# A diffusion step of two layers on one core: one half of the first layer's gate g1 summed on VectorE during the input product

## The chip, the core and the metric

The kernel runs on one core of a Trainium2 chip. The core has TensorE (PE in the rows: matmuls; PEld is its weight load), VectorE (DVE), ScalarE (ACT), GpSimd (POOL) and SyncE (SP, which here issues nearly all loads). The metric is the device time of one execution in microseconds (us), as a median over runs. The rows of a profile call a place in the program by its line (L431 is line 431 of the kernel) and a tile by its name in the code.

## The reference, cut to what matters

Two groups of 128 tokens (context and latent, 256 columns in all) go through two layers of width 2048. Each layer has a mixer and a gated feed-forward part, and each of the two is modulated by vectors made from a conditioning vector (`c_ctx` for context, `c` for latent):

```
adaln(cvec, w, b) = silu(cvec) @ w + b            # w_ada[l]: 2048 x 12288
sh1, sc1, g1, sh2, sc2, g2 = split(adaln(...), 6) # 2048 each, once for c_ctx, once for c
h = rmsnorm(x) * (1 + sc1) + sh1
x = x + g1 * mixer(h)                             # layer 0: attention and a bidirectional scan
h = rmsnorm(x) * (1 + sc2) + sh2
x = x + g2 * conv_ffn(h)
```

In layer 0 the mixer is an input product (`h @ w_in`, 2048 x 6592), eight heads of differential attention, sixteen heads of an RWKV-7 scan in both directions, and an output product. What is changed is where the first 1024 of the 2048 values of layer 0's `g1` are summed. They are first used after the scan, in the residual of the output product.

## The kernel before, in words

**Products.** Every large product runs in `gemm`: a weight tile is loaded by SP into one of seven `raw` buffers (512 KB a load), ScalarE copies it to the high part of a `wbt` slot (L192), VectorE subtracts to get the low part (L194), and TensorE makes three matmuls for each 128 output channels (L252, L254, L255). There are four `wbt` slots, and a slot holds two steps of k where a group is 512 wide. A *turn* is one step of k: twelve matmuls in such a group. After each turn `gemm` calls a function `fill`.

**Gate vectors.** `w_ada` is 2 x 2048 x 12288, and each of the twelve segments is made in parts. After the input modulation, a part is a *half* of 1024 values. Both ways of making a half load sixteen tiles of 128 x 1024 (one for each step of k) into the same `raw` buffers.

- `ada_pe` lets TensorE do it: four matmuls per tile (L431), 64 in a half. The profile records each as two instructions, so a half is 128 records.
- `ada_vec` lets VectorE do it: two multiply-adds per tile into the tile `av` (L454 for the first tile, L456 for the other fifteen), then eight matmuls with a selector (L464, sixteen records) that sum over the partitions.

Both end in a transpose and an addition of the bias (L470, L482). The table `AS_VEC` names the halves that go the second way. One generator, `ada_gen`, walks a fixed list (`ada_order`): for layer 0 after the first modulation it is both halves of g1, then sc2, sh2, g2. `ada_step` advances it by one step, so the halves are made strictly in that order, at whatever pace the place that calls it sets.

**Order of the work around the change.** Layer 0's input product has a first part (`gemm_joint`, nine groups, with the modulation made beside it) and a second part (`gemm(p_in, ...)`, six groups of sixteen turns, 96 turns). In the second part the groups kb, vb and r come out through `in_evac`, and the attention heads and the normalisation `kk_norm` are small tasks that `step_tasks` advances by one piece each turn. Then comes the scan: `scores` for each pair of heads and direction, `solve(b)` for four batches (a triangular inverse by many small VectorE instructions and small matmuls), `apply`, and `post`. Here `scan_fill` calls `ada_step` at half a step each round until sh2 is done, and at five steps each round once the last scores are out. The last stretch of the scan, ahead of the output product, holds `solve(3)`, `subln` (the attention heads' normalisation, L1390 to L1401), and `post(1)` (L1351 to L1377). In `solve`, the tile `Xc` (L1207) ends a long run of VectorE instructions, and the matmuls of L1216 read it. Later, `fill_out` and `fill0` advance the generator in the output product and in the feed-forward part.

The program is written in one order, and a scheduler with a cost model places the instructions of each engine. So a change in one place can reorder others.

## Time and profile before

| what | value |
|---|---|
| median of three runs | 2709.16 us (2708.67 to 2729.94) |
| the profiled execution's own time | 2707.69 us |
| its span | 2705.6 us |
| PE, DVE, ACT, POOL busy in the span | 2615.6, 2020.5, 1258.5, 298.7 us |
| granted TensorE clock, mean | 0.977 |
| second part of the input product | 269 to 425 us |
| scan, to the start of the output product | 425 to 716 us |
| output product | 716 to 820 us |
| feed-forward part of layer 0 | 820 to 1580 us |

A row of a table by stretches gives the stretch, its length, then for each engine the busy time and the count of instructions, then the granted clock (1.00 is full), the share of time in which the DMA engines were busy, and GB/s. A row of a group gives line, engine, operation, tiles (output, then inputs), shape and count, then total busy us and the mean ns of one, then the idle time just before these instructions and what ended most of it. A row of the chain of waits gives when a piece began, how long it held the chain, and what it was. Durations of matmuls that follow each other overlap, so a group's busy time, not its mean, is what the engine spends on it.

### The profile page before, as it was taken

What the parts mean: (1) busy time and instruction counts of PE and PEld (TensorE: products, weight loads), DVE (VectorE), ACT (ScalarE), POOL (GpSimd) and SP (SyncE); (2) the same over time, 40 slices, a digit from 0 to 9 for tenths busy, and PEclk for the clock granted to TensorE, in tenths of its full rate; (3) what the DMA queues carried; (4) which work ended last, traced back from release to release, by engine and by line L of the source; (5) the groups of instructions that cost most, each with busy time, mean ns of one, the idle gap of its engine ahead of it and who ended that gap; (6) DMA issues with size and microseconds to landing.
All of it is one profiled execution on the core that took longest, in us unless ns stands there. A gap on an engine that the chain in (4) does not pass through costs nothing.

```text
span 2705.6 us, 60522 instructions
## 1 busy us (share of the span) xinstructions
PE 2615.6 (97%) x24347; PEld 2443.4 (90%) x24347; DVE 2020.5 (75%) x3468; ACT 1258.5 (47%) x2074; POOL 298.7 (11%) x313
## 2 busy tenths in 40 slices
PE   6999998999999999999999989999999999999998
PEld 5889996667898999999999989978889999999998
DVE  3457765767579998978999989996479985566655
ACT  3335654554345444434444454346344454355544
POOL 2000012011100000000000047653200000000000
PEclk8999999999799999999999989999999999999999
DMA  9997656655356887877878857865798876666653
GB/s 293 304 272 209 204 169 217 243 193 199 129 189 195 257 268 240 286 249 247 277 247 267 274 169 246 275 229 177 243 299 277 258 234 195 195 195 193 194 190 119
DMA packets 446969, 616.59 MB, mean 228 GB/s; under 512 B 33461, under 2 KB 317464, under 8 KB 446048
## 3 DMA queue, kind: packets, MB, share of 16 engines
q1 hardware_dynamic: 442288, 600.83, 70.2%
q0 software_dynamic: 3040, 6.57, 0.7%
q10 hardware_dynamic: 1360, 5.33, 0.5%
q8 instruction: 191, 3.13, 0.5%
q14 instruction: 90, 0.74, 0.1%
HBM read 604.75 MB, written 7.86 MB: 226 GB/s over the span
## 4 chain that ended last, share of the span: by engine, by line
PE 84%; DVE 7%; DMA 6%; ACT 1%; issue 1%; SPq 0%; POOL 0%; DVEq 0%; ACTq 0%; POOLq 0%
PE mm L255 22%; PE mm L252 22%; PE mm L254 22%; PE ada L431 4%; DVE cu L1655 3%; DMA raw<-in_w_ada 2%; DMA raw<-in_w_in 2%; PE mm L1087 1%; DVE wbt L194 1%; DMA raw<-in_w_up 1%; PE mm L304 1%; PE mm L306 1%; PE mm L305 1%; PE mm L1648 1%; PE mm L1120 1%
## 5 line engine op out<-in xcount | busy, mean ns | idle before, releaser
L192 ACT ACTIVATE wbt<-raw 128x1024 fp32r<-128x1024 f32 (+3 forms) x768 | 793.7, 1037 | 1035.4 <-PE mm L254 696.8
L252 PE MATMUL mm<-hbt,wbt 128*128 128x256 f32 x3888 | 1086.5, 282 | 6.0 <-ACT hbt L585 2.3
L254 PE MATMUL mm<-hbt,wbt 128*128 128x256 f32 x3888 | 1081.5, 280 | 2.7 <-DVE hbt L587 2.7
L194 DVE TENSOR_TENSOR wbt<-raw,wbt 128x1024 fp32r<-128x1024 f32 (+1 forms) x688 | 812.6, 1188 | 357.7 <-ACT wbt L192 345.5
L255 PE MATMUL mm<-hbt,wbt 128*128 128x256 f32 x3888 | 1064.2, 280 | 3.5 <-DVE wbt L194 3.3
L252 PEld LDWEIGHTS mm<-hbt,wbt 128*128 128x128 f32 x3888 | 733.3, 189 | 20.3 <-issue 9.2
L254 PEld LDWEIGHTS mm<-hbt,wbt 128*128 128x128 f32 x3888 | 734.0, 189 | 6.9 <-DVE hbt L587 4.7
L255 PEld LDWEIGHTS mm<-hbt,wbt 128*128 128x128 f32 x3888 | 723.2, 189 | 9.7 <-DVE wbt L194 4.7
L254 PE MATMUL mm<-u,wbt 128*128 128x256 f32 x1344 | 371.0, 278 | 0.0
L252 PE MATMUL mm<-u,wbt 128*128 128x256 f32 x1344 | 370.9, 278 | 0.0
L255 PE MATMUL mm<-u,wbt 128*128 128x256 f32 x1344 | 365.7, 278 | 0.0
L456 DVE SCALAR_TENSOR_TENSOR av<-raw,silu_c,av 128x1024 f32<-128x1024 f32 x270 | 337.2, 1278 | 29.6 <-DMA raw<-in_w_ada 29.5
L194 POOL TENSOR_TENSOR wbt<-raw,wbt 128x1024 fp32r<-128x1024 f32 x80 | 193.5, 2427 | 909.8 <-DMA raw<-in_w_pw 800.2
L252 PEld LDWEIGHTS mm<-u,wbt 128*128 128x128 f32 x1344 | 252.2, 188 | 0.4 <-issue 0.4
L254 PEld LDWEIGHTS mm<-u,wbt 128*128 128x128 f32 x1344 | 252.0, 188 | 0.4 <-issue 0.4
L255 PEld LDWEIGHTS mm<-u,wbt 128*128 128x128 f32 x1344 | 249.1, 188 | 0.4 <-issue 0.4
L431 PE MATMUL ada<-raw,silu_c 128*32 128x256 f32 (+2 forms) x2688 | 166.0, 337 | 31.3 <-DMA raw<-in_w_ada 15.6
L1655 DVE SCALAR_TENSOR_TENSOR cu<-mm,vec,cu 128x256 f32<-128x256 f32 x428 | 174.4, 470 | 2.2 <-ACT cu L1639 1.0
L1544 DVE SCALAR_TENSOR_TENSOR cv<-mm,vec,cv 128x254 f32<-128x254 f32 x344 | 147.3, 474 | 11.8 <-ACT cv L1539 11.8
L431 PEld LDWEIGHTS ada<-raw,silu_c 128*32 128x32 f32 x2688 | 70.3, 112 | 91.7 <-issue 26.2
L304 PE MATMUL mm<-hbt,wbt 128*128 128x256 f32 x304 | 91.7, 302 | 1.9 <-DVE qkv L311 1.0
L1539 ACT ACTIVATE cv<-mm,vec 128x256 f32<-128x256 f32 x172 | 72.0, 474 | 45.9 <-PE mm L255 45.8
(449 smaller groups left out, 2889.6 us busy)
## 6 DMA issues: line engine op xcount, KB each, us to landing
raw<-in_w_ada SPq DMA_DIRECT2D x384, 512.0 KB, 5.3
raw<-in_w_up SPq DMA_DIRECT2D x688, 256.0 KB, 4.2
raw<-in_w_down SPq DMA_DIRECT2D x168, 512.0 KB, 5.0
raw<-in_w_pw SPq DMA_DIRECT2D x128, 256.0 KB, 4.3
raw<-in_w_in SPq DMA_DIRECT2D x128, 192.0 KB, 6.1
raw<-in_w_in SPq DMA_DIRECT2D x48, 512.0 KB, 3.9
raw<-in_w_out SPq DMA_DIRECT2D x32, 512.0 KB, 4.0
raw<-in_w_pw SPq DMA_DIRECT2D x32, 512.0 KB, 4.7
```

The lines of the kernel that those rows point to most:

```text
L192: act.activation(w[:, 0, 0:na * n], v, AF.Copy)
L194: pl.lo(pl.count).tensor_tensor(out=w[:, 1, 0:na * n], in0=v, in1=w[:, 0, 0:na * n].bitcast(F32), op=ALU.subtract)
L252: pe.matmul(ps, lhsT=hi, rhs=r[:, 0:TT], start=(ki == 0 and (nl > 0 or j % 2 == 0)), stop=False, skip_group_check=True)
L254: pe.matmul(ps, lhsT=hi, rhs=r[:, TT:2 * TT], start=False, stop=False, skip_group_check=True)
L255: pe.matmul(ps, lhsT=lo, rhs=r[:, 0:TT], start=False, stop=(ki == nk - 1), skip_group_check=True)
L304: pe.matmul(ps, lhsT=hi, rhs=r[:, 0:TT], start=(i == 0), stop=False, skip_group_check=True)
L305: pe.matmul(ps, lhsT=hi, rhs=r[:, TT:2 * TT], start=False, stop=False, skip_group_check=True)
L431: pe.matmul(ps[32 * j:32 * j + 32, 0:nb * 32], lhsT=silu_c[:, kt, :], rhs=rv[:, j], start=(kt == 0), stop=(kt == KT - 1))
L456: dve.scalar_tensor_tensor(out=av[:, s], in0=raw, scalar=sc, in1=av[:, s], op0=ALU.mult, op1=ALU.add)
L1539: act.activation(o, ps, AF.Copy, scale=w(1, ct))
L1544: dve.scalar_tensor_tensor(out=o[:, :, a_], in0=v2(ps)[:, :, b_], scalar=w(k, ct), in1=o[:, :, a_], op0=ALU.mult, op1=ALU.add)
L1655: dve.scalar_tensor_tensor(out=o, in0=pads[a](k), scalar=V("w_dw", k * KT + ct), in1=o, op0=ALU.mult, op1=ALU.add)
```

## The change

`(0, "g1", 0)` joins the table `AS_VEC`, so the first half of layer 0's g1 is made by `ada_vec`. The generator now starts it in the second part of the input product: from the tenth turn on, every second turn takes one step until that half is done. The half takes 38 steps, so it runs from turn 10 to turn 84 of 96; `ada_until` after the product would finish it there if it were not done. When the scan begins, the generator stands at the second half of g1, and the scan has five halves to make in place of six.

```
-    AS_VEC = [(l, nm, i) for l, nm in ((0, "g2"), (1, "sc1"), (1, "sh1"), (1, "g2")) for i in range(2)] + [(1, "g1", 0)]
+    AS_VEC = [(l, nm, i) for l, nm in ((0, "g2"), (1, "sc1"), (1, "sh1"), (1, "g2")) for i in range(2)] + [(0, "g1", 0), (1, "g1", 0)]
...
         nrm_[0] = w1.enter_context(scoped("nrmg", 1))
-        gemm(p_in, hb, in_evac, step_tasks)
+        turns = [0]
+
+        def fill_in():
+            turns[0] += 1
+            if turns[0] % 2 == 0 and turns[0] > 8 and (0, "g1", 0) not in ada_done:
+                ada_step()
+            step_tasks()
+        gemm(p_in, hb, in_evac, fill_in)
+        ada_until(0, "g1", 0)
         drain()
```

Eight lines are added ahead of the scan's code, so L1207 before is L1215 after, and so on for every line behind it. Three places show how the instructions move.

TensorE, the last two scores of the scan, before (`X`, `W` are the inverse of batch 2; `th`, `kd`, `bk` belong to the scores; `ada` is a gate half):

```order
L431 MATMUL ada<-raw,silu_c 32x256 x9
L1282 MATMUL mm<-X_7742,W 64x64 x16
L1087 MATMUL mm<-kr,th 128x256 x4
L1087 MATMUL mm<-kr,kd 128x256 x4
L1098 MATMUL mm<-table,s0r_5212 128x128
L1101 MATMUL mm<-table,bk 128x128
L1102 MATMUL mm<-table,bk 128x128
L431 MATMUL ada<-raw,silu_c 32x256
L1291 MATMUL mm<-W,X_7742 64x64 x16
```

The same place after:

```order
L1290 MATMUL mm<-X_7819,W 64x64 x16
L1095 MATMUL mm<-kr,th 128x256 x4
L1095 MATMUL mm<-kr,kd 128x256 x4
L1106 MATMUL mm<-table,s0r_5289 128x128
L1109 MATMUL mm<-table,bk 128x128
L1299 MATMUL mm<-W,X_7819 64x64 x16
L1110 MATMUL mm<-table,bk 128x128
```

Ten gate matmuls are gone from here. The gate halves of the scan are the same sequence shifted by one, so up to this place both kernels have a gate half at the same spots, and it is the last 64 matmuls that are missing.

TensorE, around the first matmuls that read `Xc` of the last `solve`, before (`sq`, `ones` are `subln`; `y`, `ex` belong to `post` and `subln`):

```order
L1390 MATMUL mm<-ones,sq 128x2 x4
L1351 MATMUL mm<-y,table 128x256
L431 MATMUL ada<-raw,silu_c 32x256 x8
L1390 MATMUL mm<-ones,sq 128x2 x4
L431 MATMUL ada<-raw,silu_c 32x256 x12
L1216 MATMUL mm<-Xc,W 32x16 x32
L858 MATMUL mm<-table,ex 128x128 x2
L1360 MATMUL mm<-table,sq 128x2 x2
L1351 MATMUL mm<-y,table 128x256
L431 MATMUL ada<-raw,silu_c 32x256 x4
L1229 MATMUL mm<-Gc,P_8629 16x16 x32
```

The same place after:

```order
L1398 MATMUL mm<-ones,sq 128x2 x4
L1224 MATMUL mm<-Xc,W 32x16 x32
L1359 MATMUL mm<-y,table 128x256
L1398 MATMUL mm<-ones,sq 128x2 x4
L1237 MATMUL mm<-Gc,P_8606 16x16 x32
L858 MATMUL mm<-table,ex 128x128
L1368 MATMUL mm<-table,sq 128x2 x2
L1359 MATMUL mm<-y,table 128x256
```

The first L1351 and the second four of L1390 stood ahead of the readers of `Xc` and now stand behind them (as L1359 and L1398).

VectorE at the same time, before (`Xc` is the tile waited for, `rn` a norm of `subln` that needs ScalarE in between):

```order
L1194 TENSOR_TENSOR ft<-G,M_8547 128x512
L1353 SCALAR_TENSOR_TENSOR y<-mm,y 128x256
L1197 TENSOR_REDUCE G<-ft 128x8x8
L1201 TENSOR_SCALAR G_8599<-G,table 128x16x16
L1393 TENSOR_SCALAR rn<-mm 128x16
L1204 STREAM_TRANSPOSE Gc<-G_8599 128x16x2x16
L1395 RECIPROCAL rn<-rn 128x16
L1207 STREAM_TRANSPOSE Xc<-Gc 128x512
L1224 COPY P_8629<-mm 32x256
```

The same place after:

```order
L1202 TENSOR_TENSOR ft<-G,M_8563 128x512
L1205 TENSOR_REDUCE G<-ft 128x8x8
L1209 TENSOR_SCALAR G_8585<-G,table 128x16x16
L1212 STREAM_TRANSPOSE Gc<-G_8585 128x16x2x16
L1215 STREAM_TRANSPOSE Xc<-Gc 128x512
L1333 TENSOR_TENSOR y<-mm,y 128x256
L1338 TENSOR_TENSOR so<-mm,Sp 64x64 x2
```

L1353, L1393 and L1395 stood ahead of `Xc` and now stand behind it, and so do two of the four updates of `y` and `so` (L1325 and L1330 before). In turn four low parts of weights (L194) stand ahead of `Xc` where there were three.

In the second part of the input product, VectorE gets sixteen pairs of `av` among the low parts of the weights, SP gets sixteen loads of `w_ada` among those of `w_in` and of the attention caches, and TensorE gets the eight selector matmuls in the last group. The last matmuls of the attention heads stand at the same place among the product's as before.

## Prediction

> **What bounds the kernel now.** I read the page first: the busy times and the chain of waits (the work that ended last, followed back).
>
> ```profile
> span 2705.6 us, 60522 instructions
> ...
> PE 2615.6 (97%) x24347; PEld 2443.4 (90%) x24347; DVE 2020.5 (75%) x3468; ACT 1258.5 (47%) x2074; POOL 298.7 (11%) x313
> ...
> PE 84%; DVE 7%; DMA 6%; ACT 1%; issue 1%; SPq 0%; POOL 0%; DVEq 0%; ACTq 0%; POOLq 0%
> PE mm L255 22%; PE mm L252 22%; PE mm L254 22%; PE ada L431 4%; DVE cu L1655 3%; DMA raw<-in_w_ada 2%; DMA raw<-in_w_in 2%; PE mm L1087 1%; DVE wbt L194 1%; DMA raw<-in_w_up 1%; PE mm L304 1%; PE mm L306 1%; PE mm L305 1%; PE mm L1648 1%; PE mm L1120 1%
> ```
>
> TensorE is busy nearly all the time and holds the chain for 84% of the span; the gate matmuls (L431) alone hold 4%. On the average any matmul taken away should pay. But averages don't say what the removed ones are worth, so I look at the two stages that the change touches. First the price of a half on either engine, from the groups by shape (all of TensorE):
>
> ```profile
> L431 PE MATMUL ada<-raw,silu_c 128*32 128x256 f32 x1408 | 119.5, 405 | 11.0 <-DMA raw<-in_w_ada 10.3 <-DVE atr L470 0.6
> ...
> L464 PE MATMUL ada<-av,sel 128*32 128x256 f32 x144 | 11.1, 388 | 0.0
> ```
>
> and the groups of VectorE from 900 to 1150 us, where the feed-forward part makes halves this way:
>
> ```profile
> L456 DVE SCALAR_TENSOR_TENSOR av<-raw,silu_c,av 128x1024 f32<-128x1024 f32 x67 | 83.7, 1277 | 6.4 <-DMA raw<-in_w_ada 6.4
> ...
> L454 DVE TENSOR_SCALAR av<-raw,silu_c 128x1024 f32<-128x1024 f32 x4 | 2.8, 738 | 0.0
> ```
>
> On TensorE a half is 128 records of 119.5 / 1408 = 0.085 us, 10.9 us. In the new form TensorE still does 16 records of 11.1 / 144 = 0.077 us, 1.2 us, and VectorE gets 30 x 1.277 + 2 x 0.738 = 39.8 us.
>
> **What is added: the input product.** Stretches of the trace (its second part without its first turns, the densest 110 us of that, and two stretches of the feed-forward part that make halves on VectorE):
>
> ```profile
> 285.00:425.00 140.00, 140.00 (x1171) 137.66 (x1173) 84.17 (x149) 72.62 (x141) 18.08 (x43) 1.00 0.59 168
> 300.00:410.00 110.00, 110.00 (x915) 107.87 (x914) 70.81 (x125) 59.01 (x112) 11.43 (x29) 1.00 0.61 175
> 900.00:1150.00 250.00, 250.00 (x2128) 247.65 (x2127) 229.15 (x287) 117.63 (x160) 0.00 (x0) 1.00 0.83 262
> 1200.00:1250.00 50.00, 48.00 (x401) 47.15 (x400) 42.24 (x48) 19.97 (x23) 0.00 (x0) 1.00 0.79 249
> ```
>
> TensorE is busy 140.00 of 140 us, so the 1.2 us of L464 lie on the path: +1.2. VectorE goes from 84.17 to 124 us of 140, 89%. At 900 to 1150 us it is busy 229.15 of 250, 92%, with the same rhythm (one `av` instruction every second turn, one low part every second turn), and TensorE loses nothing. That row is nearest, so I take 0 for the contention. The other bound is the row from 1200 us, where TensorE lost 2.00 of 50 us: 2.00 / 50 x 140 = 5.6 us. What hides the 39.8 us are the four `wbt` slots of two turns each: 1171 records in 140 us are 0.12 us each, a turn of twelve 1.4 us, so the split may be 11.5 us late. If that is used up, each further `av` costs its 1.28 us. An `av` also waits in VectorE's queue for its load, with low parts of weights queued behind it; in 250 us these waits were 6.4 us (the L456 row), and TensorE stayed at 250.00.
>
> The sixteen loads (512 KB each, 8.4 MB) fill the DMA share, 0.59 at 168 GB/s, by 60 GB/s to about 0.8, under the 0.83 of 900 to 1150 us: 0. On SP's queue they stand among the loads of the attention caches (L758), which wait for attention matmuls and hold back all loads behind them; that is the rival below. POOL is moved past nothing. L470 and L482 run on VectorE in the last turns and nobody waits for them before the scan's end.
>
> **What is removed: the end of the scan.** Since the sequence of halves is shifted by one, the missing matmuls are the last 64, all after 650 us. The chain of waits there (x18 are 18 records):
>
> ```profile
> 650.37 1.41 PE ada L431 x18
> ...
> 656.19 0.55 PE ada L431 x2
> ...
> 669.27 1.00 PE ada L431 x16
> ...
> 673.61 1.00 PE ada L431 x16
> ...
> 677.08 1.28 ACT L1394
> ...
> 678.62 0.25 DVE rn L1395
> 678.87 0.58 DVE Xc L1207
> ...
> 679.50 1.19 PE mm L1216 x64
> ...
> 681.40 0.58 PE mm L1351 x2
> 681.97 1.01 PE ada L431 x8
> ...
> 684.75 0.65 PE mm L1360 x4
> 685.40 1.86 PE ada L431 x16
> 687.26 2.16 PE mm L1216 x64
> ...
> 691.41 1.50 PE mm L1390 x8
> ...
> 714.50 0.85 PE mm L1351 x2
> ...
> 715.78 0.21 PE mm L252
> ```
>
> and VectorE's timeline ahead of `Xc` (start, us, and in brackets the idle time before):
>
> ```profile
> 663.13 1.23 DVE L194 TENSOR_TENSOR wbt<-raw,wbt 128x1024 fp32r<-128x1024 f32 x1
> ...
> 666.78 0.41 DVE L1325 TENSOR_TENSOR y<-mm,y 128x256 f32<-128x256 f32 x1
> 667.11 0.45 DVE L1330 TENSOR_TENSOR so<-mm,Sp 64x64 f32<-64x64 f32 x2
> ...
> 675.17 0.42 DVE L1353 SCALAR_TENSOR_TENSOR y<-mm,y 128x256 f32<-128x256 f32 x1
> ...
> 676.79 1.06 DVE L1204 STREAM_TRANSPOSE Gc<-G 128x512 f32<-128x512 f32 x1
> 678.62 0.25 DVE L1395 RECIPROCAL rn<-rn 128x16 f32<-128x16 f32 x1 [0.78 <-ACT rn L1394]
> 678.79 0.65 DVE L1207 STREAM_TRANSPOSE Xc<-Gc 128x512 f32<-128x512 f32 x1
> ```
>
> Up to the last scores the gate matmuls are on the path: 1.41 + 0.55 = 1.96 us. From there to `Xc` the stage is VectorE's: the last `solve` runs as one unbroken row of instructions, and the gate matmuls of 669 to 677 us fill time in which TensorE would otherwise wait for `Xc`. They are worth 0 there. The new order shortens VectorE's row: two pairs of L1325 and L1330 go behind (0.8 each, 1.6), L1353 goes (0.4), and the wait for L1395 goes (`Gc` ends at 677.85, `Xc` starts at 678.79: 0.9), while one more L194 comes (1.2). That is 1.7 us. So `Xc` comes 1.96 + 1.7 = 3.7 us earlier.
>
> Behind `Xc` the granted clock decides (stretches of 5 us; the second column of numbers is TensorE's busy time, the third last is the clock):
>
> ```profile
> 675.00:680.00 5.00, 2.67 (x61) 1.58 (x62) 3.48 (x8) 2.93 (x6) 0.52 (x2) 1.00 1.02 406
> 680.00:685.00 5.00, 5.00 (x129) 3.76 (x124) 2.23 (x6) 1.97 (x5) 0.92 (x4) 0.68 1.05 386
> 690.00:695.00 5.00, 5.00 (x80) 4.21 (x79) 2.98 (x6) 3.18 (x7) 2.21 (x6) 0.50 0.49 181
> ...
> 715.00:720.00 5.00, 5.00 (x41) 4.85 (x40) 2.32 (x6) 2.33 (x6) 0.29 (x1) 0.91 0.00 0
> ```
>
> After the thin stretch at 675 to 680 us (2.67 busy of 5) the clock falls to half at about 681.8 us and stays there until the output product begins. L1216 takes 1.19 us before and 2.16 after the fall. TensorE works without a gap in this stretch, so here it is the bound, at half speed. By parts:
> - the 24 gate records gone from it: -1.01 - 1.86 = -2.9;
> - the first L1351 and the second L1390, which stood ahead of `Xc`, now run here: +0.85 + 1.50 = +2.35;
> - the clock falls earlier, since nothing fills the time before `Xc`: the work of 679.50 to 681.97 at half speed costs 0 to 2.3; I take +1.8, near the upper end, since the gap grows;
> - L1395 with its 1.28 us of ScalarE (L1394) now lies between L1390 and L858: 0 to 1.5, I take +0.7;
> - L1360 and L1351 come forward from the output product: 0.65 + 0.85 here, about half of it back at full speed there: +0.75.
>
> Together +2.7. The end of the scan is worth -3.7 + 2.7 = -1.0 us, between -4.0 (clock and L1395 at their lower ends, 2.5 less, and 0.5 for rounding) and +0.6.
>
> [...]
>
> Sum: +1.2 + 0 - 1.0 = +0.2 us on the profiled execution's own 2707.69, 2707.9. The median of the runs shown, 2709.16, lies 1.5 above that execution, so the forecast is 2709.4 us. From the output product on, both kernels do the same work in almost the same order: 0.
>
> **The rivals.**
> - *The freed time is paid in full*: TensorE holds 84% of the chain, the later stages absorb nothing, and all 128 records count: -10.9 + 1.2 = -9.7, 2699.5 us. For it speaks the first page; against it the rows at 669 to 677 us, which lie beside VectorE's work.
> - *The weights come late in the input product (slower)*: the cache loads on SP already wait (the queue's own waits, 285 to 430 us):
>
> ```profile
> SPq L758 <- PE mm L824: 8.3, 4, 3.9
> ```
>
>   With VectorE at 89%, the attention pieces that free these buffers come later, and the `w_in` loads behind them too. It decides once the split is more than 11.5 us late. The price is up to 8.3, if these waits reach TensorE once, plus 5.6 for the contention: 13.9, which gives 2723. Against it: in the densest 110 us VectorE would need 70.81 + 39.8 = 110.6, full but not far over, and the last attention matmuls keep their place.
> [...]
>
> That the change does not do what it says I exclude: the order of the instructions shows the half moved.
>
> **How the numbers follow.** Forecast 0.55 (its own range 2705 to 2715), paid in full 0.2, late weights 0.2 (spread over 2712 to 2723), clock 0.05. The range 2699 to 2718 leaves out the clock, the upper half of the late weights and a little of the full pay, together under 0.2. A measurement of this kernel can tell about 1% (27 us) from no change. Faster by over 1% needs more than all the gains together: 0.01. Slower by over 1% needs most of the 39.8 us of VectorE on the path: 0.02. Within 1%: 0.97.
>
> **What would show it.** Right: TensorE still 140 of 140 us in the input product with VectorE near 124; L431 with 1280 records in place of 1408; `Xc` some 3.7 us earlier against the last scores' place less what the input product adds; the clock at 0.50 from well before the first L1216 reader; the output product beginning within 2 us of before. Wrong: idle time of L252 to L255 put down to L194 or to `raw<-in_w_in` between 285 and 425 us (late weights), or an output product that begins 8 us or more earlier (full pay), or a clock of 1.00 between 690 and 710 us.

## The result, and the profile after

The changed kernel takes 2735.25 us (median, 2729.06 to 2759.87), the kernel before 2709.16. The ratio on record is 1.0077, with a 95% interval of 1.0048 to 1.0106 (the quotient of the two medians is 1.0096): slower by 0.8 to 1.0%. Disturbed runs are left out of all ratios here. The profiled execution takes 2733.12 us. From its page:

```profile
span 2731.3 us, 60324 instructions
...
PE 2618.5 (96%) x24235; PEld 2452.1 (90%) x24235; DVE 2054.2 (75%) x3500; ACT 1259.4 (46%) x2074; POOL 300.0 (11%) x313
```

The groups of the gate matmuls, by shape:

```profile
L431 PE MATMUL ada<-raw,silu_c 128*32 128x256 f32 x1280 | 107.1, 396 | 13.7 <-DMA raw<-in_w_ada 13.1 <-DVE atr L470 0.6
...
L464 PE MATMUL ada<-av,sel 128*32 128x256 f32 x160 | 12.8, 388 | 0.0
```

TensorE's work hardly changed (2618.5 us busy, 2615.6 before). The span grew by 25.7 us. Where, is seen by cutting both executions at the same places of the program: the input product's second part, the scan up to the last matmuls of L1087, and from there to the output product. First before, then after (the second number after the stretch's length is TensorE's busy time, the third last the clock):

```profile
269.12:424.77 155.65, 155.65 (x1297) 152.81 (x1295) 98.53 (x184) 83.00 (x164) 19.25 (x44) 1.00 0.62 183
275.00:325.00 50.00, 50.00 (x408) 48.35 (x407) 36.81 (x80) 29.79 (x68) 4.36 (x8) 1.00 0.66 194
424.77:654.68 229.91, 221.66 (x2970) 153.50 (x2971) 154.22 (x398) 116.75 (x315) 28.54 (x76) 0.99 0.62 209
654.68:715.43 60.75, 57.84 (x802) 45.14 (x799) 36.32 (x84) 25.90 (x53) 9.03 (x26) 0.72 0.58 213
```

```profile
267.58:443.80 176.22, 160.53 (x1313) 155.97 (x1311) 134.87 (x220) 83.22 (x164) 19.20 (x44) 0.95 0.68 208
443.80:674.17 230.37, 220.95 (x2952) 153.12 (x2953) 154.25 (x398) 117.14 (x315) 28.36 (x76) 0.99 0.61 206
674.17:743.78 69.61, 61.46 (x698) 53.42 (x695) 36.92 (x84) 26.36 (x55) 9.43 (x27) 0.56 0.21 72
```

The input product is 20.6 us longer, the scan 9.3 (0.5 + 8.8). The product begins 1.5 us earlier, so the output product begins 28.4 us later; 2.7 us come back behind it, which wasn't followed up.

**The input product.** TensorE does 4.9 us more work (160.53 - 155.65) and idles 15.7 (176.22 - 160.53). By stretches of 10 us of the changed kernel, all idle time lies in one place (the last row is one of the undisturbed ones):

```profile
285.00:295.00 10.00, 9.20 (x72) 8.39 (x71) 9.68 (x10) 5.80 (x11) 0.00 (x0) 1.00 0.90 302
295.00:305.00 10.00, 0.00 (x0) 0.00 (x0) 9.95 (x23) 2.72 (x12) 1.80 (x3) 0.67 0.81 245
305.00:315.00 10.00, 5.62 (x27) 5.66 (x28) 4.59 (x12) 1.22 (x3) 0.00 (x0) 0.50 0.20 61
...
345.00:355.00 10.00, 10.00 (x88) 10.00 (x87) 9.89 (x18) 6.33 (x15) 1.27 (x2) 1.00 0.67 199
```

The waits of 280 to 325 us name it, and VectorE's timeline shows what stood ahead:

```profile
PE mm L816 <- DVE a L810: 15.2, 1, 15.2
...
ACT e L800 <- DVE mx L796: 6.2, 1, 6.2
```

```profile
295.53 0.68 DVE L795 TENSOR_REDUCE mx<-mm 128x2 f32<-128x512 f32 x1
...
297.72 2.47 DVE L456 SCALAR_TENSOR_TENSOR av<-raw,silu_c,av 128x1024 f32<-128x1024 f32 x2
...
302.03 0.16 DVE L796 TENSOR_SCALAR mx<-mx 128x4 f32<-128x4 f32 x1
...
304.66 2.47 DVE L456 SCALAR_TENSOR_TENSOR av<-raw,silu_c,av 128x1024 f32<-128x1024 f32 x2
...
308.89 0.74 DVE L810 SCALAR_TENSOR_TENSOR a<-e,sm,a 128x128 f32<-128x128 f32 x2
```

An attention head goes back and forth between VectorE (L796), ScalarE (L800) and VectorE (L808, L810), and TensorE then transposes its result (L816). L796 needs 0.16 us, and its input is ready at 296.2; it runs at 302.0, behind `av`, a low part of weights and results of kb. L810 follows at 308.9. All product matmuls behind L816 in TensorE's order stop with it, though their weights lie ready (in the whole product TensorE waits for a weight once, 0.5 us). In VectorE's queue L796 was held 5.8 us with nothing else missing. The wait costs a second time: the clock is at 0.67 in the 10 us without a matmul, and at 0.50 from 305 to 315 us. The 4.9 us of extra work are the selector matmuls (1.2 by the prediction's price) and this half clock. The scheduler did not keep the half to the tenth turn and later, either: its first pair of `av` runs at 269.3 us, in the product's second turn.

**The end of the scan.** The same cut by 5 us, then ScalarE's timeline, then TensorE's, all of the changed kernel:

```profile
675.00:680.00 5.00, 2.84 (x37) 2.28 (x35) 3.76 (x8) 2.80 (x4) 0.00 (x0) 1.00 0.68 283
680.00:685.00 5.00, 4.65 (x23) 3.76 (x24) 2.15 (x8) 1.01 (x4) 0.52 (x1) 0.57 0.00 0
...
735.00:740.00 5.00, 5.00 (x35) 4.25 (x34) 1.59 (x3) 1.01 (x2) 0.59 (x2) 0.50 0.00 0
740.00:745.00 5.00, 4.69 (x27) 3.89 (x26) 3.29 (x9) 2.18 (x5) 1.59 (x5) 0.79 0.18 52
```

```profile
677.75 2.15 ACT L1166 ACTIVATE f<-W 32x512 f32<-32x512 f32 x2 [0.48 <-PE mm L1299]
679.93 0.37 ACT L1112 ACTIVATE s0T<-mm,th 128x128 f32<-128x128 f32 x1
```

```profile
680.35 0.53 PE L1123 MATMUL mm<-s0T,kr 128*128 128x128 f32 x2 [2.51 <-ACT s0T L1112]
...
690.37 1.12 PE L1326 MATMUL mm<-W,sf 128*64 128x128 f32 x8 [1.99 <-ACT sf L1320]
...
710.67 0.48 PE L858 MATMUL mm<-table,ex 128*128 128x128 f32 x1 [1.76 <-POOL ex L857]
```

Before, ScalarE made `s0T` ahead of `f`:

```profile
656.23 0.37 ACT L1104 ACTIVATE s0T<-mm,th 128x128 f32<-128x128 f32 x1 [2.75 <-PE mm L1102]
...
658.92 2.19 ACT L1158 ACTIVATE f<-W 32x512 f32<-32x512 f32 x2 [0.48 <-PE mm L1291]
```

Now `f` (2.15 us, of the last `solve`) stands ahead of it, and L1110, the last of the three transposes ahead of `s0T`, stands behind the 32 records of L1299. TensorE waits 2.51 us for `s0T`, no gate matmul fills the gap, and the clock falls at the last scores. It stays at half for some 61 us, to 742, where it was 34 us before (682 to 716).

### The profile page after: what moved, and what is told of

Read it like the earlier page. It is cut to its first block, busy times and chain, and to the rows that moved or that the text cites. A ratio compares the mean times of both kernels' runs of the same rounds, so it can differ in the third digit from the quotient of the medians.

```text
span 2731.3 us, 60324 instructions
## 1 busy us (share of the span) xinstructions
PE 2618.5 (96%) x24235; PEld 2452.1 (90%) x24235; DVE 2054.2 (75%) x3500; ACT 1259.4 (46%) x2074; POOL 300.0 (11%) x313
## 4 chain that ended last, share of the span: by engine, by line
PE 86%; DMA 6%; DVE 5%; ACT 1%; issue 1%; SPq 0%; DVEq 0%; POOL 0%; ACTq 0%
PE mm L252 22%; PE mm L254 22%; PE mm L255 22%; PE ada L431 4%; DMA raw<-in_w_ada 3%; DVE wbt L194 2%; PE mm L1095 1%; DMA raw<-in_w_in 1%; DMA raw<-in_w_up 1%; PE mm L304 1%; PE mm L306 1%; PE mm L305 1%; PE mm L1656 1%; DVE av L456 1%; PE mm L1128 1%
## 5 line engine op out<-in xcount | busy, mean ns | idle before, releaser
L252 PE MATMUL mm<-hbt,wbt 128*128 128x256 f32 x3888 | 1088.2, 283 | 6.0 <-ACT hbt L585 2.3
L255 PE MATMUL mm<-hbt,wbt 128*128 128x256 f32 x3888 | 1067.8, 281 | 4.1 <-DVE wbt L194 4.1
L194 DVE TENSOR_TENSOR wbt<-raw,wbt 128x1024 fp32r<-128x1024 f32 (+1 forms) x688 | 812.7, 1189 | 331.6 <-ACT wbt L192 319.5
L252 PEld LDWEIGHTS mm<-hbt,wbt 128*128 128x128 f32 x3888 | 736.6, 190 | 20.9 <-issue 9.5
L255 PEld LDWEIGHTS mm<-hbt,wbt 128*128 128x128 f32 x3888 | 726.4, 190 | 9.7 <-DVE wbt L194 5.5
L456 DVE SCALAR_TENSOR_TENSOR av<-raw,silu_c,av 128x1024 f32<-128x1024 f32 x300 | 374.5, 1280 | 41.0 <-DMA raw<-in_w_ada 40.7
L252 PE MATMUL mm<-u,wbt 128*128 128x256 f32 x1344 | 371.2, 278 | 0.0
L255 PE MATMUL mm<-u,wbt 128*128 128x256 f32 x1344 | 365.9, 278 | 0.0
L194 POOL TENSOR_TENSOR wbt<-raw,wbt 128x1024 fp32r<-128x1024 f32 x80 | 193.6, 2426 | 910.9 <-ACT wbt L192 908.4
L252 PEld LDWEIGHTS mm<-u,wbt 128*128 128x128 f32 x1344 | 252.3, 188 | 0.4 <-issue 0.4
L254 PEld LDWEIGHTS mm<-u,wbt 128*128 128x128 f32 x1344 | 252.1, 188 | 0.4 <-issue 0.4
L255 PEld LDWEIGHTS mm<-u,wbt 128*128 128x128 f32 x1344 | 249.2, 188 | 0.4 <-DVE wbt L194 0.4
L431 PE MATMUL ada<-raw,silu_c 128*32 128x256 f32 (+2 forms) x2560 | 154.5, 332 | 34.3 <-DMA raw<-in_w_ada 19.5
L431 PEld LDWEIGHTS ada<-raw,silu_c 128*32 128x32 f32 x2560 | 67.2, 114 | 90.1 <-DMA raw<-in_w_ada 27.2
```

Source lines behind the costliest of these rows:

```text
L194: pl.lo(pl.count).tensor_tensor(out=w[:, 1, 0:na * n], in0=v, in1=w[:, 0, 0:na * n].bitcast(F32), op=ALU.subtract)
L252: pe.matmul(ps, lhsT=hi, rhs=r[:, 0:TT], start=(ki == 0 and (nl > 0 or j % 2 == 0)), stop=False, skip_group_check=True)
L254: pe.matmul(ps, lhsT=hi, rhs=r[:, TT:2 * TT], start=False, stop=False, skip_group_check=True)
L255: pe.matmul(ps, lhsT=lo, rhs=r[:, 0:TT], start=False, stop=(ki == nk - 1), skip_group_check=True)
L431: pe.matmul(ps[32 * j:32 * j + 32, 0:nb * 32], lhsT=silu_c[:, kt, :], rhs=rv[:, j], start=(kt == 0), stop=(kt == KT - 1))
L456: dve.scalar_tensor_tensor(out=av[:, s], in0=raw, scalar=sc, in1=av[:, s], op0=ALU.mult, op1=ALU.add)
```

## The experiments

The table puts the traces side by side, in us. Input: the second part of the input product. The next three columns count from the scan's first gate matmul: to the end of the last scores (their last matmul), to the first reader of the last `Xc`, to the output product. All are worked out from TensorE's timelines. Ratio: time against the kernel before, with its interval. Each trace is one execution; in one set of 31 executions the kernel before took 2699.58 to 2742.41 us, so a trace's columns and the ratio need not agree to some 10 us.

| kernel | input | last scores | Xc | output | ratio |
|---|---|---|---|---|---|
| before | 155.6 | 236.8 | 254.7 | 290.7 | 1 |
| changed | 176.2 | 241.7 | 259.6 | 300.0 | 1.0077 (1.0048 to 1.0106) |
| give_room | 178.4 | 239.0 | 254.9 | 294.3 | 1.0112 (1.0041 to 1.0183) |
| no_loads | 190.9 | 238.0 | 254.0 | 294.2 | one time, 2735.85 us |
| twice_as_fast | 187.1 | 241.3 | 254.0 | 301.4 | one time, 2764.97 us |
| late_start | 161.8 | 252.1 | 268.0 | 307.6 | 1.0062 (1.0036 to 1.0088) |
| swap_half | 176.8 | 249.0* | 267.0* | 304.3* | 1.0026 (0.9991 to 1.0060) |
| late_swap | 160.4 | 248.6 | 265.4 | 306.1 | 1.0037 (1.0000 to 1.0074) |
| late_even | 169.6 | 238.2 | 256.1 | 293.5 | 1.0025 (0.9986 to 1.0063) |
| copies_first | 178.2 | 232.7 | 255.6 | 290.6 | 1.0061 (1.0022 to 1.0100) |
| combo | 166.4 | 231.6 | 249.6 | 289.0 | 1.0031 (0.9995 to 1.0066) |
| more_halves | 155.6 | 249.7* | 268.4* | 308.8* | 1.0033 (0.9987 to 1.0078) |
| warm_once | 155.6 | 249.9* | 267.9* | 303.0* | 0.9984 (0.9946 to 1.0022) |
| rate4 | 155.6 | 234.8 | 250.3 | 286.4 | 0.9960 (0.9925 to 0.9996) |
| rate4_again | 155.6 | 232.6 | 246.6 | 289.9 | 0.9957 (0.9914 to 1.0001) |
| late_rate4 | 160.4 | 233.9 | 249.8 | 289.0 | 1.0018 (0.9986 to 1.0049) |

In the rows with a star the clock also fell to half in mid-scan for some 27 us, which costs about 13 us (to the last scores 249.9 in warm_once, 236.8 before; last section); their later columns are read less 13.

### The input product: place, load or transfers?

**give_room.** Is it the place of L816 in TensorE's order?

```
-            yield
+            for _ in range(7 if h == 3 else 1):
+                yield
             ps = bank()
             for i in range(3):
                 pe.transpose(ps[:, i * P:(i + 1) * P], ...
```

> The changed kernel, but one head's attention (the fourth) waits 12 turns longer in program order between making its weights a on VectorE and turning them on TensorE: L816 stands at turns 32 and 33 of the input product on TensorE where it stood at 16 to 17.6. VectorE's work is the same, all is computed. Theory A (TensorE stops because this matmul stands in its fixed order ahead of weights that VectorE reaches 15 us later): the wait of 15.2 us for a goes, the half clock after it too, the scan begins at 425 to 430 us instead of 443.8, and the execution takes 2714 to 2720 us, since the end of the scan stays as in the changed kernel. Rival B (VectorE's 40 us cost TensorE some 18 us in the input product wherever the attention matmul stands, through late weights or buffers): waits of the same sum turn up elsewhere between 280 and 440 us, 2728 to 2735 us.

Measured: 178.4 us. The one wait of 15.2 became two, 8.5 and 7.6 us, both again for `a` (by the same matmul, L817 in this kernel), ending at 327 and 336 us. So theory A in this form falls. VectorE is behind by about 15 us, and TensorE meets that at the next thing VectorE owes it.

**no_loads.** VectorE's time, or the sixteen loads?

```
-            raw, nxt = nxt, (load(kt + 1) if kt < KT - 1 else None)
+            raw, nxt = nxt, (nxt if (l, nm, b0) == (0, "g1", 0) else
+                             load(kt + 1) if kt < KT - 1 else None)
```

> The changed kernel, but the half that VectorE makes in the input product reads its first load sixteen times: 15 of its 16 loads (7.9 MB) are left out, and the gate it makes is not the reference's. VectorE's instructions are the same in number and size. Theory A2 (VectorE's time): TensorE still waits 10 to 18 us for a in the first third of the input product, which takes 172 to 178 us (176.2 in the changed kernel). Rival B (the loads: raw buffers and transfers that the weights lack): the wait is gone, 156 to 162 us.

The waits of 280 to 330 us:

```profile
PE mm L816 <- DVE a L810: 22.7, 2, 15.7
```

Without the loads it is worse, 190.9 us, with a longer wait than expected. The loads aren't the cause (rival B falls). But this kernel changed more than the loads: its VectorE instructions are the same in number and not in place. First the changed kernel, then no_loads:

```profile
L456 DVE SCALAR_TENSOR_TENSOR av<-raw,silu_c,av x30: 1271/1280/1287, 280.6 to 388.3; 128x1024 f32<-128x1024 f32 x30
```

```profile
L456 DVE SCALAR_TENSOR_TENSOR av<-raw,silu_c,av x30: 1253/1276/1282, 269.3 to 328.2; 128x1024 f32<-128x1024 f32 x30
```

The same thirty instructions lie within 59 us in place of 108, denser than in twice_as_fast below (279.2 to 353.4). So 190.9 us belongs with the dense cases, and the loads with VectorE's load held fixed were not tested.

**twice_as_fast and late_start.** The dose: all 40 us of VectorE in half the turns, or at the old pace in a later place.

```
-            if turns[0] % 2 == 0 and turns[0] > 8 and ...
+            if turns[0] > 8 and ...                           # twice_as_fast
+            if turns[0] % 2 == 0 and turns[0] > 32 and ...    # late_start
```

> The changed kernel, but a step in every turn from turn 10 on, not in every second; all is computed. Theory A2 (local overload of VectorE): over 275 to 325 us VectorE would get 36.8 + 0.91 x 50 = 82 us of work for 50, so TensorE waits 25 to 35 us instead of 15.2 in the input product, again for a or for weights, and the product takes 184 to 196 us. Rival B (the place of one attention matmul in the fixed order, not the load, sets the loss): the wait stays between 12 and 18 us, 173 to 179 us.

> The changed kernel, but the half's steps begin behind turn 32 of the input product instead of behind turn 8, at the same pace; all is computed. Theory A2 (VectorE is overloaded locally: between 275 and 325 us it had 36.8 us of other work before, and one step of 1.28 us every second turn of 1.4 us adds 0.46 x 50 = 22.8, together 59.6 us for 50; TensorE waits for the first thing VectorE owes it, wherever that stands): from turn 32 on VectorE had 63 us in the last 110, with the half 103, so the wait of 15 us is gone, the input product takes 156 to 161 us (155.6 before, 176.2 in the changed kernel) and the scan begins near 427. The end of the scan stays at 294 to 300 us from its first gate matmul, since its fillers are still missing: 2712 to 2720 us where no other fall of the clock lies in the scan. Rival B (any 40 us of VectorE in this part costs TensorE some 18): input product 172 to 178 us.

The waits of twice_as_fast (270 to 350 us), then two stretches of late_start, then one of combo, which starts behind turn 36 with three steps in four turns:

```profile
PE mm L816 <- DVE a L810: 22.5, 3, 21.1
```

```profile
264.19:426.00 161.81, 157.41 (x1313) 153.03 (x1311) 135.33 (x222) 83.99 (x166) 25.75 (x49) 1.00 0.72 227
304.00:354.00 50.00, 50.00 (x415) 48.94 (x414) 45.90 (x69) 26.05 (x48) 3.62 (x6) 1.00 0.74 237
```

```profile
316.00:376.00 60.00, 55.53 (x464) 54.38 (x462) 59.96 (x83) 31.41 (x62) 2.35 (x4) 1.00 0.83 265
```

The input product grows with the density: 155.6 without the half, 160.4 to 161.8 late and slow, 166.4 and 169.6 late and denser, 176.2 as in the change, 187.1 at twice its pace. With VectorE at 45.90 of 50 us TensorE lost nothing (50.00 busy); at 59.96 of 60 it lost 4.5 (55.53 busy). So A2 holds: it is the local overload, met through the attention's chain. Whether the order on VectorE alone would do, with the attention's short instructions put ahead of `av`, was not tried. A turn takes 155.65 / 96 = 1.62 us, so one step of 1.277 us every second turn is 0.39 us per us. Between 275 and 325 us VectorE had 36.81 us of 50 before; with 19.7 more it needs 56.5. (The expectations used 1.4 us a turn and came to 59.6, a little much.) The whole of late_start was not cured: its input product is just over the 156 to 161 us expected, the scan takes 307.6 where 294 to 300 were expected, and the time is 2730.91 us for 2712 to 2720. Six steps were left behind the last turn. In the scan's first 60 us TensorE idles 12.1 us (7.8 before), mostly where gate matmuls wait for their own loads, and the clock is at half there for some 17 us. combo's input product missed its 157 to 161 us as well (166.4).

### The end of the scan: fillers, clock or order?

**swap_half.** The gate matmuls are given back to the scan's end.

```
-    AS_VEC = [... for i in range(2)] + [(0, "g1", 0), (1, "g1", 0)]
+    AS_VEC = [... for i in range(2) if (l, nm, i) != (0, "g2", 0)] + [(0, "g1", 0), (1, "g1", 0)]
...
-                if (0,"sh2") not in ada_done:                            # scan_fill; step_late likewise
+                if (0,"g2",0) not in ada_done:
```

> The changed kernel, but the first half of g2 is taken off VectorE and made on TensorE during the scan in return (the scan runs on until that half is done). All is still computed. The order of TensorE's instructions over the scan's last 300 rows is then the one of the kernel before, with as many gate matmuls as before; the input product is that of the changed kernel. Theory A (two separate losses: some 19 us in the input product, some 9 at the end of the scan because the filling gate matmuls are missing there): the scan's first gate matmul still comes at about 444 us, from there to the output product it takes 290.7 us as before (300.0 in the changed kernel), the profiled execution takes 2723 to 2727 us. Rival B (the end of the scan is later only because the whole scan starts later and meets other transfers): 300 us for that stretch, 2733 us.

304.3 less 13 for the fall in mid-scan is 291.3, 290.7 before: with TensorE's order as before, the end of the scan is as before, in spite of the late start. Rival B falls. The input product keeps its loss (176.8). The ratio, 1.0026, is smaller than 21 us in the input product would make it, even at the interval's upper end of 1.0060; the traced execution took 2747.98 us, against a median of 2717.61, and the difference was left open.

**late_swap and late_even.** Both remedies, at two paces.

```
-            if turns[0] % 2 == 0 and turns[0] > 8 and ...
+            if turns[0] % 2 == 0 and turns[0] > 32 and ...    # late_swap, with the lines of swap_half
+            if turns[0] % 4 != 3 and turns[0] > 36 and ...    # late_even, with the lines of swap_half
```

> The changed kernel with both remedies: the half's steps behind turn 32, and the first half of g2 on TensorE in the scan in return; all is computed. If the two losses are independent (theory A2 with A), both go: input product 156 to 161 us, the scan's first gate matmul to the output product 289 to 293 us less any fall of the clock in mid-scan, within 5 us of the kernel before, 2702 to 2714. If the scan's end depends on more than the number of fillers (rival C), that stretch stays at 296 us or more.

> The changed kernel with the half's steps behind turn 36 of the input product, three in four turns, so that no rest of them is left behind the last turn; and the first half of g2 on TensorE in the scan in return. TensorE's order in the scan is then that of the kernel before, but for a few places behind the last Xc, and s0T stands ahead of f. All is computed. Theory A2: input product 156 to 161 us. Theories A and C both: the last L1087 to the output product 60 to 63 us; the whole within 0.3% of the kernel before. Rival: if the moved half costs something else in the scan (other transfers, later buffers), the stretch from the scan's first gate matmul to the output product stays over 295 us where the clock doesn't fall in mid-scan.

late_swap missed: 306.1. Some 9 us of it lie in the scan's first part, as in late_start (TensorE waits 17.8 us in the first 215 us, 8.2 before). But from the last scores on it is some 4 us longer too (57.5 against 53.9), though it has 128 gate records behind the last L1087 where there were 110; `s0T` stands behind `f` there, with a wait of 2.0 us. In late_even `s0T` stands ahead, and the scan takes 293.5. So the number of fillers alone doesn't decide, and the order came under suspicion. The input product of late_even missed its 156 to 161 us, for it is the denser pace again.

**copies_first, combo and rate4.** The order alone: priority for the copies of the last scores, in the changed kernel (copies_first) and with the later pace too (combo); and the kernel before with a slower pace, where `s0T` falls behind `f` by itself (rate4).

```
+            with tc.high_priority(800 if (ct, d) == (7, 1) else 0):
+                act.activation(s0T, ...), act.activation(bht, ...), act.activation(kh, ...)
                                            # and so for the transposes; copies_first, combo
-        rate = [5]
+        rate = [4]                          # rate4, on the kernel before
```

> The changed kernel, but the transposes and copies of the last scores (s0T, bh, kh) get priority, so that ScalarE makes s0T ahead of f and no longer behind it (in the kernel before it stood ahead too). No gate matmul is added: none are left at the end of the scan, as in the changed kernel. All is computed. Theory C (at the end of the scan the order on ScalarE does the damage: TensorE waits 2.5 us for s0T, the clock falls there and stays at half from the last scores on): the wait for s0T is gone, the clock falls some 12 us later after the last scores, and from the last L1087 to the output product it takes 60 to 64 us (60.75 before, 69.6 in the changed kernel). Theory A (the missing filling matmuls do it): 67 to 70 us, clock at half as early as in the changed kernel. The input product is the changed kernel's, 176 us.

> The changed kernel with the half's steps behind turn 36 in three of four turns, and s0T ahead of f; no half of g2 in return, so the end of the scan has no filling gate matmul. All is computed. If theories A2 and C both hold, this is the change without its two losses: input product 157 to 161 us, from the last L1087 to the output product 58 to 63, 2699 to 2712 us, which may be faster than the kernel before by up to 0.3%. If theory A (fillers) holds, 67 to 70 us for the second and 2712 to 2720.

> The kernel before, with the pace of the gate steps in the scan set to 4 in place of 5 per ten rounds; nothing is moved to VectorE, all six halves are made in the scan, and 64 gate matmuls stand behind the last scores (55 before). The scheduler then places s0T behind f on ScalarE, as in the changed kernel. All is computed. Theory C (the order of s0T and f): TensorE waits 2 us or more for s0T, the clock falls at the last scores, and from the last L1087 to the output product it takes 66 to 71 us, 60.75 before, in spite of all the fillers. Theory A (fillers): 59 to 63 us.

TensorE's timeline of combo, where the last scores no longer wait:

```profile
659.86 1.73 PE L1301 MATMUL mm<-W,X 64*64 64x64 f32 x26
661.51 0.49 PE L1125 MATMUL mm<-s0T,kr 128*128 128x128 f32 x2
```

Without one filler more, the scan goes from 300.0 to 290.6 and 289.0, the level of before. By the column of the last scores the order is worth 9 to 10 us (241.7 against 232.7 and 231.6), but less than 5 of that at `s0T` itself: from the last L1087 to the end of the last scores it takes 11.3 us in the changed kernel, 6.6 in these two and 6.8 before. The rest lies ahead, since the priorities changed TensorE's order from some 130 us into the scan on. How much of the 4.5 us comes from `s0T` behind `f`, and how much from L1110 behind L1299, wasn't separated. The expected mark, last L1087 to output product, came out at 64.5 and 64.0, about the top of C's 60 to 64, because that L1087 itself came some 4 us earlier.

The clock sided with theory A, though. From the end of the last scores to the output product, before, changed, copies_first and combo:

```profile
661.53:715.43 53.90, 50.99 (x733) 39.80 (x733) 31.60 (x77) 22.05 (x47) 9.03 (x26) 0.69 0.55 199
```

```profile
685.50:743.78 58.28, 52.64 (x630) 46.30 (x629) 29.93 (x68) 22.55 (x48) 8.91 (x26) 0.51 0.17 56
```

```profile
678.72:736.62 57.90, 51.16 (x627) 44.06 (x625) 31.05 (x75) 22.17 (x47) 9.09 (x26) 0.53 0.18 58
```

```profile
664.36:721.76 57.40, 51.55 (x632) 44.88 (x631) 32.08 (x77) 22.90 (x49) 9.43 (x27) 0.55 0.18 56
```

With `s0T` in time, the clock falls some 3 to 4 us behind the last scores all the same, in copies_first during this wait, which gate records filled before:

```profile
683.59 1.12 PE L1328 MATMUL mm<-W,sf 128*64 128x128 f32 x8 [3.13 <-ACT sf L1322]
```

It stays at half for 58 and 51 us. So the missing fillers still cost some 4 us behind the last scores, and these two kernels reach the level of before by what they gain ahead of the last L1087 (226.1 and 225.0 us into the scan, 229.9 before). twice_as_fast, which has no gate matmul there either, takes 60.1 us; before, swap_half, late_even and warm_once, which have theirs, take 53.2 to 55.3. (In the kernels not named, other work lies ahead of that mark or more work behind it, so they don't compare.)

rate4 refutes C as it stood: from the last L1087 to the output product it takes 61.4 us, as theory A had it. TensorE does wait for `s0T`, and the clock falls, but it is back ten us later:

```profile
652.54 0.49 PE L1115 MATMUL mm<-s0T,kr 128*128 128x128 f32 x2 [1.64 <-ACT s0T L1104]
...
659.49 3.64 PE L431 MATMUL ada<-raw,silu_c 128*32 128x256 f32 x32
```

```profile
655.00:660.00 5.00, 5.00 (x30) 3.76 (x33) 2.20 (x8) 2.31 (x5) 0.00 (x0) 0.50 0.73 277
...
665.00:670.00 5.00, 4.69 (x51) 3.52 (x46) 4.12 (x12) 1.17 (x3) 1.19 (x3) 1.00 0.93 311
...
685.00:690.00 5.00, 3.94 (x88) 3.02 (x86) 2.84 (x7) 3.77 (x8) 2.19 (x5) 1.00 0.94 312
```

Full clock follows 32 gate records in a row. In the second trace of this kernel (rate4_again, below) the wait for `s0T` is much the same, 1.63 us, but the clock does not fall there; it falls 17 us behind the last scores and then stays at half for 37 us. So both of the changed kernel's losses at the scan's end are real, about 4.5 us up to the end of the last scores by order and 4.4 behind it where the fillers are missing; how much late fillers give back differs from trace to trace, and late_swap isn't explained.

**warm_once and more_halves.** What holds the clock? The first adds four matmuls of 128x256 in the gap ahead of the last `Xc`, the second 256 real gate records around it.

```
+                if b == 3 and q0 == 0:                                       # warm_once
+                    for _ in range(4):
+                        pe.matmul(b2[q0][:, 0:256], lhsT=ident, rhs=G2[:, 0:8] ..., start=True, stop=True)
-    AS_VEC = [... for l, nm in ((0, "g2"), (1, "sc1"), ...) ...]            # more_halves, and the scan runs
+    AS_VEC = [... for l, nm in ((1, "sc1"), ...) ...]                        # until g2 is done, not sh2
```

> The kernel before, with four matmuls added that compute nothing used (identity by G2, 128x256, about 0.5 us each) on TensorE where it waits 2.33 us for the last Xc; their place is behind G2. Theory A (the granted clock falls to half at 681.8 us because of that gap of 2.3 us, and stays there for 34 us): without the gap the clock stays at 1.00 past 682 us, at least up to the next wait of 2 us or more; the output product begins 5 to 16 us earlier than 290.7 us after the scan's first gate matmul, 2692 to 2703 us. Rival B (the clock falls because the small matmuls of the last solve, 16 to 32 rows and columns, use little of TensorE, gap or no gap): it falls at 682 to 686 us all the same, output product at the same time within 2 us, 2706 to 2710 us.

> The kernel before, with both halves of g2 made on TensorE, during the scan's end and the output product, in place of VectorE in the feed-forward part; all is computed. 256 gate records more, 21.8 us at full clock, of which some 170 lie between the last Xc and the output product and fill its waits. Theory A (filling matmuls keep the clock up): the granted clock in the stretch from 682 us to the output product is 0.8 or more, that stretch takes at most 5 us longer than the 34 us of before in spite of 14 us more matmul work, and the execution takes 2700 to 2715 us. Rival B (the clock at this place is not set by how TensorE is filled): 0.50 all through, the stretch is 25 us or more longer, 2725 to 2745 us.

warm_once: the gap is closed, the clock holds only some 5 us longer (it falls at about 699 us, some 275 after the scan's start, less 13 that is 262; before 257), and the output product comes at 303.0 - 13 = 290.0, 0.7 earlier. That is rival B's outcome: with the gap closed, the clock still falls in the last `solve`, so the gap was not what made it fall. more_halves, stretches of the trace:

```profile
705.00:710.00 5.00, 5.00 (x97) 2.44 (x97) 1.09 (x4) 0.62 (x2) 0.53 (x2) 0.50 0.68 230
710.00:715.00 5.00, 5.00 (x103) 3.85 (x103) 2.49 (x5) 3.09 (x7) 1.74 (x4) 0.98 0.82 287
```

The clock falls, but is back at 710 us and stays: about 17 us at half in place of 34, and the stretch is 5 us longer (308.8 - 13 - 290.7) for 166 records more, 14 us at full clock. That is theory A, with the clock at 0.79 in the mean from the last `Xc` to the output product (0.8 expected). It doesn't pay (2722.39 us, for 2700 to 2715 expected), since the rest of the two halves then lies in the output product, and from its start to the feed-forward part's first down product it takes 13 us more.

**warm_all** (18 such matmuls through the last `solve`, in the kernel before) had no clear outcome:

> The kernel before, with 18 matmuls that compute nothing used (identity by G2 or y, 128x256) among the last solve's matmuls, two or three ahead of each group of small ones. [...] Rival B (dense matmuls in this number don't move the clock): 0.50 all through, 18 x 1 us more at half clock, 300 us or more.

The clock fell some 7 us earlier than before, at a wait of 1.8 us for a gate load, came back, and fell again, 34 us at half in all as before; the scan took 305.6 us in that trace, yet the time over all runs was the same as before (0.9992, 0.9949 to 1.0035).

### The kernel before at a slower pace, and the moved half at that pace

rate4 once more, and the changed kernel at that pace:

```
-            if turns[0] % 2 == 0 and turns[0] > 8 and ...
+            if turns[0] % 2 == 0 and turns[0] > 24 and ...    # late_rate4, with the priorities of copies_first
-        rate = [5]
+        rate = [4]                                             # rate4_again, late_rate4
```

> The kernel before with the pace of the gate steps in the scan at 4 in place of 5, once more, for the interval and a second trace. If the first result (0.996) is real: ratio 0.993 to 0.999, from the scan's first gate matmul to the output product about 286 us, with a clock that comes back to 1.00 between the last scores and the last Xc, where 64 gate matmuls are left. If it was scatter: ratio 0.998 to 1.003.

> The changed kernel with the half's steps behind turn 24, every second turn, and the scan's pace at 4; priority for the last scores' copies is asked for, but s0T stands behind f all the same, and no gate matmul is left behind the last scores. All is computed. If the moved half has a gain of its own (some 5 us ahead of the last Xc) that outlives the half clock behind it: input product 158 to 166 us, scan to output product 285 to 290 us, 2700 to 2712 us, at best even with rate4. If the fillers are worth more at the scan's end than the half saves: 292 us or more, and slower than rate4 by 6 us or more.

rate4, the kernel before with one number changed, is the best tried: 0.9960 and 0.9957, about 11 us under the kernel before and 1.2% under the changed one (0.996 / 1.0077). One interval ends just under 1 and the other just over it, so that it beats the kernel before is likely and not certain. Its scan is 1 to 4 us shorter in the traces (289.9 us in the second, for 286 expected); the rest may be the mid-scan fall of the clock, which neither of its traces shows. late_rate4 starts the moved half behind turn 24 and has rate4's pace in the scan. It still takes 160.4 us for the input product, 4.8 more than before, with a scan no shorter than rate4's. Its median of 2728.46 us missed the 2700 to 2712 expected and is 20.7 us above that of rate4_again in the same set of runs. None of the kernels with the moved half came out under the kernel before.

## Why the prediction was wrong

- **The contention in the input product** (forecast 0, other bound 5.6) is the step that failed most; it measured 19.4 with the half clock, without L464. Two choices made it. VectorE's load was taken as a mean of 140 us (124 of 140), from 285 us on; the row of L456 starts at 281, and the dense 50 us begin at 275, with 36.81 of 50 taken already. The stretch called the densest 110 us (300 to 410, 70.81 us of VectorE) was not the densest either: 272 to 382 us has 74.6. And the row held nearest, 900 to 1150 us, has about the same rhythm but no attention heads, so VectorE owes TensorE other work there.
- **"The four `wbt` slots hide 11.5 us"** (with a turn of 1.4 us; it takes 1.62): nothing contradicts it for weights, for which TensorE waited 0.5 us once in the whole product. The slots cover nothing of the attention's chain, which crosses VectorE three times.
- **The slower rival** had the right place and about the right price (2723), but the wrong mechanism: cache loads and `raw` buffers. Its premise was right, that the attention's pieces come later when VectorE is full; but TensorE itself waits for them, not the loads. The signs it named, L252 to L255 waiting for L194 or loads, don't appear beyond 0.5 us, and no_loads, without fifteen of the half's loads, waits longer. "The last attention matmuls keep their place" was true of the order and is what hurt: a matmul that keeps its place while its input comes later is a wait, of 15.2 us at L816 here.
- **Ahead of `Xc`** (forecast -3.7) the changed kernel is +4.9, the other step that failed. Of this, +0.5 lies ahead of the last L1087 and +4.5 between it and the end of the last scores, where 1.96 us were to be saved; from there to `Xc` it takes 17.9 us in both kernels. So the gate matmuls there were worth 0, as forecast, and the 1.7 us by which VectorE's row was to get shorter did not show, with the clock at half in that whole stretch of the changed kernel. What was overlooked is an order shown ahead of the prediction, L1299 before L1110; ScalarE's order, with `f` ahead of `s0T`, was not looked at. combo has -5.1, but its priorities changed the order too, so what the missing gate matmuls free by themselves isn't shown.
- **Behind `Xc`** (forecast +2.7): +4.4 in the changed kernel, +3.4 in combo. More work at half clock and an earlier fall were right in kind. The reason given for the fall in the kernel before, the thin stretch ahead of `Xc` (2.67 us busy of 5), is what warm_once speaks against. The sum for the whole end of the scan, -1.0, is near copies_first (-0.1) and combo (-1.7), but by other terms (+0.9 and -1.0 in copies_first), so that is luck. The upper bound of +0.6 doesn't follow from the terms given for it, which make +0.3.
- **The selector matmuls** (forecast +1.2, by the groups 12.8 - 11.1 = 1.7) and the 1280 records of L431 came as forecast. **VectorE's sum** came near: 134.87 - 98.53 = 36.3 us more in the product, forecast 39.8 for the whole half.
- **Paid in full** didn't happen. The 0.05 for the clock is a chance for an early return of full clock behind `Xc`; neither the trace of the kernel before nor that of the changed one shows it (at half for some 34 and 61 us). rate4 and more_halves show the clock coming back where gate matmuls are left (to 1.00 from 665 us, to 0.98 from 710 us).

## What to carry to other kernels

Before work is put on an engine with room, lay its busy time out by stretches as short as the buffers that cover it (10 to 50 us here), and look for everything that other engines wait for in its queue, not only the stream that has slots. Where a scheduler orders the engines, compare the order of all of them around the place that loses work, not only of those in the sum: here a copy and a transpose that fell behind longer work cost 4.5 us, where a gain of 2.0 was forecast. Matmuls that only fill gaps can cost time when they are taken away: without them the end of the scan took some 4 us longer here, with the clock at half for nearly all of it.

## What was not expected of the hardware

The clock can fall without any idle time of TensorE: warm_once in mid-scan, and the kernel before at the same place of the program, where TensorE ran the same instructions:

```profile
580.00:585.00 5.00, 5.00 (x122) 3.89 (x116) 3.31 (x12) 3.94 (x11) 1.05 (x3) 1.00 0.86 304
585.00:590.00 5.00, 5.00 (x39) 3.35 (x36) 4.50 (x11) 3.29 (x9) 0.00 (x0) 0.67 0.24 90
590.00:595.00 5.00, 5.00 (x42) 3.84 (x34) 0.47 (x1) 1.50 (x2) 0.00 (x0) 0.50 0.33 105
```

```profile
585.00:590.00 5.00, 5.00 (x83) 3.54 (x78) 4.91 (x14) 3.63 (x9) 0.00 (x0) 1.00 0.28 102
```

TensorE is busy 5.00 of 5 throughout; the fall comes right behind the small matmuls of a `solve` (32x32): they end at 585.3 us, and the eight records of L1087 from 586.3 us on take 1.75 us, where they took 1.13 before. It lasted some 27 us in the traces of swap_half, warm_once and more_halves, and did not come in those of before, the changed kernel, give_room, late_even and warm_all, which have the same order of TensorE's instructions up to there: this order alone does not decide it. In the nine other traces no fall of that length came there either (copies_first has one of 3.4 us). What sets it off in one trace and not in another isn't shown. That the small matmuls bring it about is a guess of ours that was not tested by itself.
